# A third plain pair ahead of the seven-product pairs of each MLP, its blocks in other PSUM banks, and a later spread of the norm's roots

## The chip, the cores and the metric

The kernel runs on one core of a Trainium2 chip. The metric is the device time of one execution in microseconds, as the median of several runs. The engines are named as in the profile: PE (matrix products), PEld (its weight loads), DVE (vector), ACT (scalar), POOL (GpSimd) and SP (which here issues the loads).

## What is computed

A residual stream of 512 tokens by 1024 features goes through two layers. The first has a gated MLP mixer (gMLP), the second a forgetting attention (FoX), and each is followed by a channel MLP with a squared ReLU. Every sub-layer begins with an RMS norm. What the change touches is the channel MLP, which runs twice:

```python
def rms_norm(x, g):
    y = x * rsqrt(mean(x * x, axis=-1) + 1e-6)
    return y * g

def sqrelu_mlp(h, w1, w2):           # h 512x1024, w1 1024x4096, w2 4096x1024
    return square(relu(h @ w1)) @ w2

x = x + sqrelu_mlp(rms_norm(x, mlp_norm_g[i]), mlp_w1[i], mlp_w2[i])
```

## The kernel before

**Precision and layout.** The stream is kept transposed, as eight tiles `x[b]` of 128 features by 512 tokens. Each operand of a product is split into a rounded high part and a low rest, and each product is three matmuls (`mm3`: high by high, high by low, low by high), accumulated in one PSUM bank. A weight chunk of 128 by 1024 (512 KB) is loaded by SP into a `raw` buffer (three of them), copied to `wh` by ACT (line 85), and the rest `wl` is made by DVE (line 86); there are four `wh`/`wl` buffers. Class `Stream` does this ahead of use: `take()` of chunk i splits up to chunk i+3 and loads up to i+6, as far as buffers are free.

**The order.** Instructions are written in program order for all engines. A scheduler at build time simulates the engines and emits, per engine, a fixed order: an instruction that is not ready in that simulation can be passed by later ones that are. `keep_in_program_order` pins an instruction, and `issue_after` puts instructions of an engine behind a given one. On the chip each engine then goes through its own order and waits on semaphores.

**The norm.** `Norm.block` (lines 267 to 277) makes the split stream `xh`, `xl` without the root, and adds up the squares on POOL. `Norm.finish` (line 290) sums over features with eight small matmuls into `nps`, DVE makes `ms` (line 297) and POOL the power -1/2, `rstd` (line 299). `Norm.spread` (line 301) broadcasts `rstd` with eight small matmuls into bank `npb`, and ACT copies it to `rbc` (line 308). Since the root is a factor per token, the up products can run before it is known; `rbc` is needed only when their banks are read.

**The MLP** (line 454). The 4096 hidden features are 32 blocks of 128, in 16 pairs. Each pair takes two chunks of `w1`. The first pairs are plain: `up(f)` runs 24 matmuls of 512 columns for a block (`dense_a`), into bank `ph`. Then `squares(n)` reads both banks of a pair with `rbc` (line 512, DVE, into `zc`, of which there is one buffer), ACT squares (line 499) and copies to `zh` (line 502), and DVE makes `zl` (line 503). All other pairs run `up_pair` (line 515), a seven-product scheme of the Strassen and Winograd kind on a 2 by 2 split of features and tokens: seven products of 12 matmuls of 256 columns, in banks `da` and `bc`. It needs sums of token halves (`token_sums`: `th` by ACT, `tl` by DVE and POOL, lines 470 to 482) and sums of the pair's weights (`Stream._sums`: `ssum` with four POOL operations at lines 112 to 115, split into `sh` by ACT and `sl` by DVE). `down_blocks` (line 549) runs 12 matmuls of 512 columns per block into bank `po` (`psB`), from the `zh`, `zl` of two pairs, and DVE adds them to `x` (line 559).

`MLP_ORDER` lists three "up" entries, then for each of the pairs 3 to 15 an "up" and two "down" chunks, whose four blocks are laid between the four parts of `up_pair`, and the remaining down chunks. PSUM has four banks `psA`, three `psB` and one `psD` (`nps`, `npb`). Before the change, two pairs are plain, all four of their blocks stand in `psA`, and pair 2 is the first `up_pair`, without down blocks between its parts:

```python
phs = [up(0), up(1)]
nm.finish()
more = [up(2, True)]
nm.spread()
more.append(up(3, True))
zs[0] = squares(0, phs)
zs[1] = squares(1, more)
```

`True` pins the first matmul of the block, and the weight sums of pair 2 are put behind the last of the token sums on POOL (`sums_behind`).

Of the kernel before, what the change touches and what calls it, by code (L numbers as in the profile page):

```python
# [1 line left out]

# [9 lines left out]
ALU = mybir.AluOpType  # L12
# [31 lines left out]

PLAIN = 2
MLP_ORDER = [("up", n) for n in range(3)]
_down = [("down", g, m) for g in range(8) for m in range(4)]
for _n in range(3, 16):  # L50
# [4 lines left out]
class Stream:  # L55
# [6 lines left out]
    def __init__(self, nc, pool, chunks, bufs, ahead, load_ahead, halved=()):  # L62
        self.nc, self.pool, self.bufs = nc, pool, bufs
        self.chunks = [c if isinstance(c, tuple) else (c, None) for c in chunks]
        self.sums_pool = self.sums_behind = None
        self.ahead, self.load_ahead = ahead, load_ahead
        self.halved = halved
        self.raw, self.parts = {}, {}
        self.loaded = self.split = self.taken = 0
# [18 lines left out]
    def _split(self):  # L88
        nc, i = self.nc, self.split
        kind = self.chunks[i][1]  # L90
        t, n = self.raw[i] if kind == "first" else self.raw.pop(i)
        hi = self.pool.tile([P, CHUNK_COLS], F32R, tag="wh", name=f"wh{i}", bufs=self.bufs[1])
        lo = self.pool.tile([P, CHUNK_COLS], F32R, tag="wl", name=f"wl{i}", bufs=self.bufs[1])
        eng = nc.gpsimd if i in self.pooled else nc.vector
        pieces = [slice(n // 2, n)] if kind == "second" else self._pieces(i, n)
        for sl in pieces:
            self._parts(hi[:, sl], lo[:, sl], t[:, sl], eng)
        self.parts[i] = (hi, lo)
        if kind == "second":
            with self.sums_behind or nullcontext():  # L100
                self._sums(i, self.raw.pop(i - 1)[0], t)
            self.sums_behind = None
        self.split += 1

    def _sums(self, i, f, g):
# [35 lines left out]
def trunk(ctx: ExitStack, tc: tile.TileContext, A, out, stages=4):  # L141
    nc = tc.nc
    pe, dve, act, pool = nc.tensor, nc.vector, nc.scalar, nc.gpsimd
# [8 lines left out]
    def psA(name):  # L152
        return ps.tile([P, S], F32, tag="A", name=name, bufs=4)
# [23 lines left out]
    def mlp_chunks(w1, w2):  # L177
        r = []
        for kind, *at in MLP_ORDER:
            if kind == "down":  # L180
                r += [w2[at[0], at[1]]]
            elif at[0] < PLAIN:
                r += [w1[2 * at[0] + e] for e in range(2)]
# [21 lines left out]
    ws = Stream(nc, wp, chunks, bufs=(3, 4), ahead=3, load_ahead=3, halved=(0, 1))  # L205
# [46 lines left out]
    def mm3(dst, ah, al, bh, bl, start, stop, pin=False, more=False):  # L252
        first = mm(dst, ah, bh, start, False, more)
        if pin:
            tc.keep_in_program_order(first)
        mm(dst, ah, bl, False, False, more)
        mm(dst, al, bh, False, stop, more)
# [52 lines left out]
    def dense_a(dst, w, nm, pin=False):  # L310

        wh, wl = (t.rearrange("p (k m) -> p k m", m=P) for t in w)
        for k in range(KB):
            mm3(dst, wh[:, k], wl[:, k], nm.h[k], nm.l[k], k == 0, k == KB - 1, pin and k == 0)
# [26 lines left out]
    nm = Norm(0)  # L341
# [8 lines left out]
    with ExitStack() as st:  # L350
# [6 lines left out]
        for g in range(4):  # L357
            pv = [(psB if g == 1 and i < 3 else psA)(f"pv{g}_{i}") for i in range(NT)]
            for c in range(4):
                wh, wl = (t.rearrange("p (k n) -> p k n", k=2) for t in ws.take())  # L360
                for i in range(NT):
                    for kk in range(2):
                        k = 2 * c + kk
# [90 lines left out]
    def mlp(nm, done):  # L454
        HS = S // 2
        with ExitStack() as st:
# [1 line left out]
            ws.sums_pool = mp  # L458
            pad(mp, 32)

            def up(f, pin=False):
                ph = psA(f"ph{nm.n}_{f}")
                dense_a(ph, ws.take(), nm, pin)
                return ph


# [3 lines left out]
            def token_sums(k):  # L470
                xg, t = (mp.tile([P, 2, S], F32, tag=f"z{w}", name=f"t{w}{nm.n}_{k}", bufs=5) for w in "hl")
                for e in range(2):
                    act.activation(xg[:, e], x[k + 4 * e], AF.Copy, scale=gains[:, nm.n, k + 4 * e : k + 4 * e + 1])
                (b11, b12), (b21, b22) = ((xg[:, e, :HS], xg[:, e, HS:]) for e in range(2))
                t = t.rearrange("p a (b n) -> p (a b) n", b=2)
                dve.tensor_tensor(t[:, 0], b12, b11, op=ALU.subtract)
                dve.tensor_tensor(t[:, 2], b22, b12, op=ALU.subtract)
                tc.keep_in_program_order(pool.tensor_tensor(t[:, 1], b22, t[:, 0], op=ALU.subtract))
                last = tc.keep_in_program_order(pool.tensor_tensor(t[:, 3], b21, t[:, 1], op=ALU.subtract))
                act.activation(th[k], t, AF.Copy)  # L480
                dve.tensor_tensor(tl[k], t, th[k].bitcast(F32), op=ALU.subtract)
                return last

            def half(e, j):
                sl = slice(j * HS, (j + 1) * HS)
# [11 lines left out]
            def rectified(n, c):  # L497

                act.activation(c, c, AF.Square)
                h = mp.tile([P, 2, S], F32R, tag="zh", name=f"zh{nm.n}_{n}", bufs=5)  # L500
                l = mp.tile([P, 2, S], F32R, tag="zl", name=f"zl{nm.n}_{n}", bufs=5)
                act.activation(h, c, AF.Copy)
                dve.tensor_tensor(l, c, h.bitcast(F32), op=ALU.subtract)
                return h, l

            def squared(n):
                return mp.tile([P, 2, S], F32, tag="zc", name=f"zc{nm.n}_{n}", bufs=1)

            def squares(n, phs):
                c = squared(n)  # L510
                for e, ph in enumerate(phs):
                    dve.scalar_tensor_tensor(c[:, e], ph, 0.0, nm.rbc, op0=ALU.max, op1=ALU.mult)
                return rectified(n, c)
# [50 lines left out]
            zs = {}  # L564
            with tc.issue_after(nm.squared.ins):
                for k in range(4):
                    last = token_sums(k)
            ws.sums_behind = tc.issue_after(last.ins)
            phs = [up(0), up(1)]
            nm.finish()  # L570
            more = [up(2, True)]
            nm.spread()
            more.append(up(3, True))
            zs[0] = squares(0, phs)
            zs[1] = squares(1, more)
            at = 2
            while at < len(MLP_ORDER):
                kind, *arg = MLP_ORDER[at]
                at += 1
# [17 lines left out]
    if stages == 1:  # L597
        for b in range(KB):
            store(b)
        return  # L600
    fx = Norm(2)
    mlp(nxt, fx.block if stages > 2 else store)
    if stages == 2:
        return
    nm = fx
# [3 lines left out]
    with ExitStack() as st:  # L609
# [277 lines left out]
        last = nx3.block if stages > 3 else store  # L887
# [16 lines left out]
    if stages == 3:  # L904
        return
    mlp(nx3, store)


# [70 lines left out]
```

## Time and profile before

| | us |
|---|---|
| median of 3 runs | 1290.82 (1290.09 to 1290.98) |
| the profiled execution | 1290.49 |
| its span, first to last instruction | 1288.8 |
| PE busy | 1263.7 |
| DVE / ACT / POOL busy | 887.4 / 631.0 / 503.4 |

The profile is of one execution. Times within it count from the first instruction. An entry of the timeline has its start, its length, the engine, the line and the operation with its output and inputs, and in brackets the idle time ahead of it with what ended it. Matmuls are pipelined, so that the length of one is more than its share of time: the spacing of the starts is what counts. PEclk is the granted clock of TensorE, 1.00 being 2.4 GHz and 0.50 being 1.2 GHz.

### The profile page before, as it was taken

Reading aid. Unit: us, or ns where it says so; the run is one execution under the profiler, and the core shown is the slowest. Engines: PE = TensorE matmul, PEld = TensorE weight load, DVE = VectorE, ACT = ScalarE, POOL = GpSimd, SP = SyncE. Lnnn points to the kernel's source line nnn. Section 1 sums busy time; section 2 is a strip of 40 time slices with the busy share of each in tenths; the row PEclk is TensorE's granted clock in tenths of the full one; section 3 lists DMA queues with packets and bytes.
Section 4 is the critical chain, followed back from the end, with each engine's and each line's share of the span. In section 5 each row is a group of like instructions: output and inputs, shape, how many; then the busy total and the mean of one; then the engine's idle time right before and its main releaser. Section 6 shows DMA issues by size and latency. Waiting matters only on the chain.

```text
span 1288.8 us, 18536 instructions
## 1 busy us (share of the span) xinstructions
PE 1263.7 (98%) x7180; PEld 1118.5 (87%) x7180; DVE 887.4 (69%) x1212; ACT 631.0 (49%) x993; POOL 503.4 (39%) x423
## 2 busy tenths in 40 slices
PE   9999999998999999999999999999979999999998
PEld 8888888887999999998899899898869999999987
DVE  7347766688767676765536777777897867676763
ACT  7334333355534343443467687678465434444430
POOL 4209423027423232210657667666284422222200
PEclk9999999998999999999999999999989999999999
DMA  7332323222332333323223222223213333232321
GB/s 249 95 115 82 91 90 85 96 83 70 105 121 85 112 95 102 104 94 95 80 83 99 82 83 74 87 78 106 77 64 116 99 98 107 90 114 83 115 82 66
DMA packets 39608, 124.02 MB, mean 96 GB/s; under 512 B 4816, under 2 KB 5840, under 8 KB 39520
## 3 DMA queue, kind: packets, MB, share of 16 engines
q1 hardware_dynamic: 39232, 122.82, 30.4%
q8 instruction: 56, 0.92, 0.3%
q14 instruction: 32, 0.26, 0.1%
q10 hardware_dynamic: 288, 0.02, 0.0%
HBM read 120.69 MB, written 2.13 MB: 95 GB/s over the span
## 4 chain that ended last, share of the span: by engine, by line
PE 85%; DVE 8%; ACT 2%; POOL 2%; issue 1%; DMA 1%; POOLq 0%; ACTq 0%; DVEq 0%
PE po L245 34%; PE da L245 12%; PE bc L245 9%; PE pq L245 8%; PE pv L245 7%; PE pu L245 7%; DVE xl L273 2%; PE pg L245 2%; PE ot L245 2%; DVE wl L86 1%; DVE ee L811 1%; PE lg L245 1%; PE tp L250 1%; PE sp L428 1%; ACT wh L85 1%
## 5 line engine op out<-in xcount | busy, mean ns | idle before, releaser
L85 ACT ACTIVATE wh<-raw 128x1024 fp32r<-128x1024 f32 (+3 forms) x230 | 219.0, 953 | 276.6 <-PE po L245 86.5
L86 DVE TENSOR_TENSOR wl<-raw,wh 128x1024 fp32r<-128x1024 f32 (+1 forms) x178 | 255.0, 1444 | 50.9 <-ACT wh L85 50.5
L245 PE MATMUL po<-zl,wh 128*128 128x512 f32 x512 | 200.5, 392 | 0.0
L245 PE MATMUL po<-zh,wh 128*128 128x512 f32 x512 | 200.2, 391 | 0.0
L245 PE MATMUL po<-zh,wl 128*128 128x512 f32 x512 | 199.5, 390 | 0.0
L559 DVE TENSOR_TENSOR x<-x,po 128x512 f32<-128x512 f32 x128 | 87.3, 682 | 111.5 <-PE po L245 111.5
L86 POOL TENSOR_TENSOR wl<-raw,wh 128x768 fp32r<-128x768 f32 (+3 forms) x52 | 103.1, 1983 | 124.2 <-ACT wh L85 121.7
L112 POOL TENSOR_TENSOR ssum<-raw 128x512 f32<-128x512 f32 x28 | 40.7, 1453 | 261.1 <-DMA raw<-in_m_dram 242.4
L85 ACT ACTIVATE sh<-ssum 128x1024 fp32r<-128x1024 f32 x56 | 59.4, 1061 | 169.5 <-POOL ssum L113 121.7
L245 PEld LDWEIGHTS po<-zh,wl 128*128 128x128 f32 x512 | 96.2, 188 | 19.6
L245 PEld LDWEIGHTS po<-zh,wh 128*128 128x128 f32 x512 | 96.5, 188 | 18.0
L245 PEld LDWEIGHTS po<-zl,wh 128*128 128x128 f32 x512 | 96.6, 189 | 16.2
L245 PE MATMUL pq<-wh,xh 128*128 128x384 f32 (+2 forms) x256 | 88.4, 345 | 0.0
L412 POOL TENSOR_SCALAR vn<-v,mv,lnr 128x128 f32<-128x128 f32 x64 | 63.3, 1004 | 59.4 <-DVE vl L416 59.3
L245 PE MATMUL pq<-wh,xl 128*128 128x384 f32 (+2 forms) x256 | 83.1, 324 | 0.0
L245 PE MATMUL pq<-wl,xh 128*128 128x384 f32 (+2 forms) x256 | 82.7, 323 | 0.0
L86 DVE TENSOR_TENSOR sl<-ssum,sh 128x1024 fp32r<-128x1024 f32 x56 | 71.5, 1277 | 11.5 <-ACT sh L85 11.5
L114 POOL TENSOR_TENSOR ssum<-raw,ssum 128x512 f32<-128x512 f32 x28 | 39.3, 1404 | 75.7 <-DVE sl L86 75.4
L115 POOL TENSOR_TENSOR ssum<-raw,raw 128x512 f32<-128x512 f32 x28 | 63.5, 2269 | 1.2 <-DVE sl L86 1.2
L245 PE MATMUL da<-th,sl 128*128 128x256 f32 x224 | 63.4, 283 | 0.0
L245 PE MATMUL da<-tl,sh 128*128 128x256 f32 x224 | 63.4, 283 | 0.0
L245 PE MATMUL da<-th,sh 128*128 128x256 f32 x224 | 63.1, 282 | 0.0
(212 smaller groups left out, 3517.9 us busy)
## 6 DMA issues: line engine op xcount, KB each, us to landing
raw<-in_m_dram SPq DMA_DIRECT2D x128, 512.0 KB, 3.6
raw<-in_gw_u_dram SPq DMA_DIRECT2D x16, 512.0 KB, 3.5
raw<-in_gw_o_dram SPq DMA_DIRECT2D x16, 512.0 KB, 3.5
raw<-in_fw_qkv_dram SPq DMA_DIRECT2D x20, 384.0 KB, 3.0
raw<-in_gw_v_dram SPq DMA_DIRECT2D x14, 512.0 KB, 3.8
raw<-in_fw_g_dram SPq DMA_DIRECT2D x8, 512.0 KB, 3.4
cb<-cd SPq DMA_DIRECT2D x16, 256.0 KB, 3.3
raw<-in_fw_o_dram SPq DMA_DIRECT2D x8, 512.0 KB, 3.5
```

The lines of the kernel that those rows point to most:

```text
L85: self.nc.scalar.activation(hi, t, AF.Copy)
L86: eng.tensor_tensor(lo, t, hi.bitcast(F32), op=ALU.subtract)
L112: tt(s12[:, 0], a21, a22, op=ALU.add)
L114: tt(s43[:, 0], a12, s12[:, 1], op=ALU.subtract)
L115: tt(s43[:, 1], a11, a21, op=ALU.subtract)
L245: ins = pe.matmul(dst, a, b, start=start, stop=stop, skip_group_check=more)
L250: placed(pe.transpose(dst, src, ident[: src.shape[0], : src.shape[0]]), 256)
L273: dve.scalar_tensor_tensor(l, x[b], gcol, h.bitcast(F32), op0=ALU.mult, op1=ALU.subtract)
L412: pool.tensor_scalar(vn[:, i], v[i][:, cb * P : (cb + 1) * P], mv[:, i, 0:1], lnr[:, i : i + 1], op0=ALU.subtract, op1=ALU.mult)
L428: pe.matmul(dst, vh[:, 2 * c + i], wide, start=True, stop=False)
L559: dve.tensor_tensor(x[b], x[b], pt, op=ALU.add)
L811: dve.tensor_scalar(ees[i], ees[i], rc[:, i : i + 1], None, op0=ALU.mult)
```

## The change

Three pairs are plain instead of two; pair 2 takes plain blocks 4 and 5 in place of the seven products, and its two weight chunks need no sums. The blocks of pair 1 (2 and 3) stand in two of the three `psB` banks, those of pairs 0 and 2 in `psA`. `finish` stays behind block 1; `spread` moves from behind block 2 to behind block 4. The pins on blocks 2 and 3 and the order between weight sums and token sums go. `squares` runs for all three pairs behind block 5. The first `up_pair` is then pair 3, which has down blocks between its parts.

```diff
-PLAIN = 2
+PLAIN = 3
...
         if kind == "second":
-            with self.sums_behind or nullcontext():
-                self._sums(i, self.raw.pop(i - 1)[0], t)
-            self.sums_behind = None
+            self._sums(i, self.raw.pop(i - 1)[0], t)
...
-            def up(f, pin=False):
-                ph = psA(f"ph{nm.n}_{f}")
-                dense_a(ph, ws.take(), nm, pin)
+            def up(f, bank):
+                ph = bank(f"ph{nm.n}_{f}")
+                dense_a(ph, ws.take(), nm)
                 return ph
...
-                last = tc.keep_in_program_order(pool.tensor_tensor(t[:, 3], b21, t[:, 1], op=ALU.subtract))
+                tc.keep_in_program_order(pool.tensor_tensor(t[:, 3], b21, t[:, 1], op=ALU.subtract))
...
-                    last = token_sums(k)
-            ws.sums_behind = tc.issue_after(last.ins)
-            phs = [up(0), up(1)]
+                    token_sums(k)
+            phs = [[up(0, psA), up(1, psA)]]
             nm.finish()
-            more = [up(2, True)]
+            phs.append([up(2, psB), up(3, psB)])
+            phs.append([up(4, psA)])
             nm.spread()
-            more.append(up(3, True))
-            zs[0] = squares(0, phs)
-            zs[1] = squares(1, more)
-            at = 2
+            phs[2].append(up(5, psA))
+            for n in range(PLAIN):
+                zs[n] = squares(n, phs[n])
+            at = PLAIN
```

## Rows read from the trace of the kernel before

**Rows 1.** The page: span, then busy time of PE, then the chain by engine.
```profile
span 1288.8 us, 18536 instructions
...
PE 1263.7 (98%) x7180; PEld 1118.5 (87%) x7180; DVE 887.4 (69%) x1212; ACT 631.0 (49%) x993; POOL 503.4 (39%) x423
...
PE 85%; DVE 8%; ACT 2%; POOL 2%; issue 1%; DMA 1%; POOLq 0%; ACTq 0%; DVEq 0%
```

**Rows 2.** Waits of PE, longest first: total us, times, longest.
```profile
PE npb L245 <- POOL rstd L299: 11.6, 2, 5.8
PE tp L250 <- DVE ptl L846: 5.1, 4, 1.9
```

**Rows 3.** Timeline of PE, first MLP.
```profile
296.03 0.95 PE L245 MATMUL nps<-ones,sqs 128*128 128x2 f32 x8
...
302.19 0.39 PE L245 MATMUL ph<-xh,wl 128*128 128x512 f32 x1
308.40 2.08 PE L245 MATMUL npb<-ident,rstd 128*128 128x128 f32 x8 [5.82 <-POOL rstd L299]
310.13 0.77 PE L245 MATMUL ph<-xh,wh 128*128 128x512 f32 x1
...
316.34 0.28 PE L245 MATMUL da<-th,wh 128*128 128x256 f32 x1
...
329.29 0.40 PE L245 MATMUL po<-zh,wh 128*128 128x512 f32 x1
```

**Rows 4.** Timeline of PE, second MLP.
```profile
954.08 0.39 PE L245 MATMUL ph<-xh,wl 128*128 128x512 f32 x1
960.27 2.07 PE L245 MATMUL npb<-ident,rstd 128*128 128x128 f32 x8 [5.81 <-POOL rstd L299]
...
968.23 0.28 PE L245 MATMUL da<-th,wh 128*128 128x256 f32 x1
...
978.41 0.28 PE L245 MATMUL da<-xh,wl 128*128 128x256 f32 x1
978.81 0.39 PE L245 MATMUL bc<-xh,sh 128*128 128x256 f32 x1
```

**Rows 5.** Stretches of the first MLP: length, busy (count) by engine, PEclk, DMA.
```profile
302.60:308.40 5.80, 0.00 (x1) 0.00 (x1) 5.22 (x5) 1.06 (x1) 5.80 (x4) 0.68 0.00 0
308.40:310.13 1.73, 1.73 (x9) 1.73 (x9) 0.85 (x1) 0.00 (x0) 1.73 (x1) 0.50 0.89 268
310.13:316.34 6.21, 6.21 (x27) 5.08 (x26) 4.30 (x4) 3.01 (x4) 4.35 (x4) 0.89 0.28 94
```

**Rows 6.** Timelines of DVE and POOL, first MLP, around the root.
```profile
303.51 0.15 DVE L297 TENSOR_SCALAR ms<-nps 128x4 f32<-128x4 f32 x1
...
304.67 2.24 POOL L113 TENSOR_TENSOR ssum<-ssum,raw 128x512 f32<-128x512 f32 x1
306.87 1.48 POOL L299 TENSOR_TENSOR rstd<-ms,mhalf 128x4 f32<-128x4 f32 x1
```

**Rows 7.** The chain in order of time: 24 matmuls of 512 and of 256 columns.
```profile
162.61 5.44 PE pu L245 x24
...
316.50 2.87 PE da L245 x24
```

**Rows 8.** Timeline of PE in the FoX stage: `npb` without a wait.
```profile
648.07 1.05 PE L245 MATMUL npb<-ident,rstd 128*128 128x128 f32 x8
648.88 0.43 PE L245 MATMUL pq<-wh,xh 128*128 128x400 f32 x1
```

**Rows 9.** Timeline of DVE, first MLP: chunk 4's rest, then the squares.
```profile
299.59 1.75 DVE L86 TENSOR_TENSOR wl<-raw,wh 128x1024 fp32r<-128x1024 f32 x1
...
314.52 1.27 DVE L512 SCALAR_TENSOR_TENSOR zc<-ph,rbc 128x512 f32<-128x512 f32 x2
318.01 1.45 DVE L503 TENSOR_TENSOR zl<-zc,zh 128x1024 fp32r<-128x1024 f32 x1 [2.22 <-ACT zh L502]
...
324.54 1.22 DVE L503 TENSOR_TENSOR zl<-zc,zh 128x1024 fp32r<-128x1024 f32 x1
```

**Rows 10.** Timeline of POOL, first MLP: the weight sums of pair 3.
```profile
311.07 1.30 POOL L112 TENSOR_TENSOR ssum<-raw 128x512 f32<-128x512 f32 x1 [0.70 <-DMA raw<-in_m_dram]
...
317.08 1.30 POOL L114 TENSOR_TENSOR ssum<-raw,ssum 128x512 f32<-128x512 f32 x1
```

**Rows 11.** Groups by line: splits of a whole chunk and of sums.
```profile
L86 DVE TENSOR_TENSOR wl<-raw,wh 128x1024 fp32r<-128x1024 f32 x146 | 227.8, 1574 | 49.8 <-ACT wh L85 49.4
...
L86 DVE TENSOR_TENSOR sl<-ssum,sh 128x1024 fp32r<-128x1024 f32 x56 | 71.5, 1277 | 11.5 <-ACT sh L85 11.5
...
L85 ACT ACTIVATE sh<-ssum 128x1024 fp32r<-128x1024 f32 x56 | 59.4, 1061 | 169.5 <-POOL ssum L113 121.7 <-issue 17.6 <-POOL ssum L112 14.2
```

More of the change, by code (lines that the diff above doesn't have):

```diff
@@ L1 @@
-from contextlib import ExitStack, nullcontext
+from contextlib import ExitStack
 import concourse.bass as bass
@@ L64, in __init__ @@
         self.chunks = [c if isinstance(c, tuple) else (c, None) for c in chunks]
-        self.sums_pool = self.sums_behind = None
+        self.sums_pool = None
         self.ahead, self.load_ahead = ahead, load_ahead
@@ L478, in token_sums @@
                 tc.keep_in_program_order(pool.tensor_tensor(t[:, 1], b22, t[:, 0], op=ALU.subtract))
-                last = tc.keep_in_program_order(pool.tensor_tensor(t[:, 3], b21, t[:, 1], op=ALU.subtract))
+                tc.keep_in_program_order(pool.tensor_tensor(t[:, 3], b21, t[:, 1], op=ALU.subtract))
                 act.activation(th[k], t, AF.Copy)
                 dve.tensor_tensor(tl[k], t, th[k].bitcast(F32), op=ALU.subtract)
-                return last
             def half(e, j):
```

## The prediction

> **What bounds the kernel now.** I read the page first. PE is busy for 1263.7 of 1288.8 us and holds 85% of the chain that ended last [rows 1]. So only two things move the time: what PE has to issue, and the some 25 us in which it stands still. The waits of PE come next: the largest is that of the `npb` matmuls on POOL's `rstd`, 11.6 us in two waits of 5.8, more than twice the next [rows 2]. The timeline of PE shows where they are, one in each MLP: the last matmul of block 2 starts at 302.19, and the eight of `npb` at 308.40 after 5.82 us idle [rows 3]; in the second MLP it is 954.08 and 960.27 [rows 4]. The reader should see that this wait has a tail. By the stretches, the granted clock falls to its lower level, 1.2 GHz, in the idle time; the `npb` matmuls run at 0.50 throughout, and block 3 at a mean of 0.89 [rows 5].
>
> Why the root is late: `nps` is issued at 296.03 [rows 3], but DVE reaches `ms` only at 303.51, behind its part of the token sums, and POOL reaches `rstd` only at 306.87, behind a weight sum that ends at 306.91, so that it is there at 308.35 [rows 6]. Nothing on PE between blocks 2 and 3 covers this.
>
> **The change, part by part.**
>
> *Later spread.* With the spread behind block 4, blocks 3 and 4 stand ahead of `npb`. Undisturbed, 24 matmuls of 512 columns take 5.44 us [rows 7], so `npb` is due at 302.42 (302.19 and one spacing of 0.227) + 2 x 5.44 = 313.30. `rstd` would have been there at 308.35 by its old path, 4.9 us before. The wait goes, and its clock tail with it. Before, from 302.42 to the first `da` matmul at 316.34, PE spent 13.92 us on `npb` and block 3 [rows 3]; the second MLP gives 968.23 - 954.31 = 13.92 too [rows 4]. Undisturbed, the same work takes 0.81 (`npb` from 648.07 to 648.88 [rows 8]) + 5.44 = 6.25 us. Gain: 7.67 us in each MLP, of which 5.82 is the wait and the rest mostly the slow clock.
>
> *Pair 2 plain.* It adds 48 matmuls of 512 columns, 48 x 0.2267 = 10.88 us, and removes 84 of 256, 84 x 2.87/24 = 10.05 us [rows 7]. Price: 0.83 us in each MLP. The shorter form is dear for its columns: 0.1196 us for 256 is more than half of 0.2267 for 512. The Trainium skill ("TensorE: Matmul & The Clock Gate", Back-to-back issue gap) gives the spacing at the full clock as columns over 2.4 GHz plus some 2.5 ns, and by it the pairs would be estimated at 10.36 and 9.17 us. The price would be 1.19, and the gain of both MLPs 0.7 us smaller; the rows differ from the page in both widths, and they decide.
>
> *Other engines.* Pair 2 loses four POOL sums, two `sh` of 1.06 us on ACT and two `sl` of 1.28 on DVE, and all that reads `da` and `bc`; it gains the second half of a `wl` split (1.57 whole) and two bank reads of 0.64 [rows 9, 11]. All three engines have less to do, and none of this sets PE's pace, so I count it as nothing. If that cover failed, it would show as the waits among the rivals. The bytes loaded and SP's issues are the same; a plain chunk gives its `raw` buffer back when it is split, where one with sums keeps it until POOL has summed, so loads can only come earlier.
>
> *Block 4's and 5's weights.* Chunk 4's `wl` was ready at 301.34 [rows 9], needed at 307.86. Chunk 5 follows it by one split, needed at 314.11. Nothing.
>
> *Banks.* Blocks 2 and 3 in `psB` leave two `psA` banks for blocks 4 and 5; the first `up_pair` needs the banks of blocks 0 and 1. Before, the first bank was read by 315.16 (one of two in 1.27 us from 314.52 [rows 9]), 5.03 us after block 3 began at 310.13 [rows 3]. Block 5 takes 5.44 us. `bc` follows `da` by 2.87 us. A margin of 0.4 us: cost nothing, and at most the 0.6 us of one read.
>
> *Pins and the order on POOL removed.* The first sums are now those of pair 3, whose second chunk comes later than the token sums end, so the removed order should not matter: nothing. Without pins, blocks 2 and 3 may fill small gaps where block 1 waits for the last `xl`; I bound that gain by a microsecond over both MLPs and count none.
>
> *Squares.* Three go through the one `zc` buffer. From the start of block 3, `zl` of pair 1 took until 324.54 + 1.22 = 325.76, so 15.6 us [rows 3, 9]. Pair 2's unfilled 10.05 us covered it. Now the first `up_pair` has down blocks in its program order, but the emitted order can leave them behind: before, even pair 3's first products were put ahead of the down blocks, whose first matmul came at 329.29, 3.5 us after `zl` was there [rows 3]. Between zero and the full wait worked out below (5.7), I take 0.3 us in each MLP, the size of the one gap there is near (978.41 to 978.81, less one spacing of 0.12 [rows 4]).
>
> *Sum.* In each MLP -7.67 + 0.83 + 0.3 = -6.54; both, -13.1 us. Against the profiled execution, 1290.49 (its span 1288.8 and 1.7 around it), that is 1277.4. The median of the runs is 0.3 above that execution, so I predict 1277.7, 1.0% faster.
>
> **Rivals.**
>
> *A. As summed.* 1275 to 1281.5: down by a microsecond or two for filled gaps, up by up to 2 us of new waits in each MLP. For it: a margin of 4.9 us on `rstd`, and the trace's order, which passes work that isn't ready.
>
> *B. The wait moves to the first down block.* If the down blocks stay in written order, the 7th matmul of the first (the first to read pair 1) is due 5.44 + 2.87 + 1.36 = 9.67 us after block 5 starts, and the chain of squares takes 15.4 to 15.6 from there: a wait of 5.7, with up to 0.8 for the clock behind it. That gives back 6.5 of 6.84, and the time is about 1290. Half of it gives 1284. For it: DVE has no idle time of weight in this stretch (5.22 of 5.80 us [rows 5]), so squares have been late there already. Against: the order of the trace, above.
>
> *C. Slower: the root behind the sums of pair 3 on POOL.* No order is written between them. Those sums ran from 311.07, when the chunk came, to 318.38 [rows 10]. If `rstd` stood behind all four with the load no earlier than before, it would end at 318.38 + 1.48 = 319.9; `npb`, due at 313.30, would wait 6.6 us and bring back the clock tail of 1.7. Each MLP would be 6.6 + 1.7 - 6.84 = 1.4 worse: 1293.7. It decides from a `rstd` that ends after 318.5 (no gain); over 0.2% slower needs 319.8. For it: `rstd` did stand behind a sum before [rows 6]. Against: `ms` is ready at 303.7, and the chunk cannot be there until its `raw` buffer is free of chunk 4, at 301.3, and loaded. The Trainium skill ("TensorE: Matmul & The Clock Gate", architectural detail on engine queues) states that ScalarE, VectorE and GpSimdE take their queues strictly in order, so a root emitted behind the sums could not pass them; no row here shows it passing.
>
> *D. The move does nothing.* The order comes from a simulation, and could put `npb` ahead of block 3 as before. Then only the price of the plain pair is left, 2 x 0.83: 1292.5, which is within 0.2%.
>
> **From cases to numbers.** About 0.2% (2.6 us) is what a measurement of this kernel can tell from no change. Chances: A 0.77; B in part (1281.5 to 1288) 0.10, B in full 0.05; C 0.05; D 0.03. Faster by over 0.2% is A and partial B, 0.87; within 0.2% is full B and D, 0.08; slower is C, 0.05. For 8 in 10 the range goes from 1275, below which little of A lies, into partial B to 1286.5; it leaves out some 0.03 below and 0.15 above.
>
> **What would show it.** In the changed profile the list of PE's waits should have no `npb` on `rstd`; the granted clock should stay at 1.00 through both starts; from the last matmul of block 2 to the first `da`, PE should take 3 x 5.44 + 0.81 = 17.1 us; `rstd` should end before block 4 does; each MLP should be some 6.5 us shorter, and all else as it was. I am wrong if a new wait of PE stands at the first `po` (B), at `npb` (C, D), or at the first `da` for a bank; or if the new emission order moves other stages, the FoX stage above all, which these sums leave alone.

## The result, and the profile after

The changed kernel takes 1277.12 us (median of four runs, 1276.96 to 1278.73) against 1290.74 (the runs of the table above and one more): a ratio of 0.9898, with a 95% interval of 0.9881 to 0.9915. Predicted were 1277.7, and 1275 to 1286.5 as the range. The profiled execution's span is 1275.3 us, 13.5 less than before.

The page after: PE is busy for 1.6 us less and the span is 13.5 shorter, so that nearly all of the gain is idle time and not work.

```profile
span 1275.3 us, 18354 instructions
...
PE 1262.1 (99%) x7108; PEld 1114.0 (87%) x7108; DVE 877.2 (69%) x1206; ACT 624.9 (49%) x981; POOL 484.7 (38%) x415
...
PE 89%; DVE 6%; ACT 2%; issue 1%; POOL 1%; DMA 1%; DVEq 0%; ACTq 0%; POOLq 0%
```

The waits of PE: `npb` on `rstd`, 11.6 us in [rows 2], is gone. A `po` that waits for `zl` is new.

```profile
PE tp L248 <- DVE ptl L843: 3.6, 4, 1.9
PE po L243 <- DVE zl L500: 1.3, 1, 1.3
```

The timeline of PE in the first MLP, which answers to [rows 3]. Blocks 3 and 4 follow block 2 without a gap; from the last matmul of block 2 and one spacing, 302.88, to the first `da` at 320.12 it is 17.24 us, where 17.1 was predicted. In the second MLP it is 17.25 us, from 946.36 to 963.61.

```profile
302.65 0.39 PE L243 MATMUL ph<-xh,wl 128*128 128x512 f32 x1
302.88 0.39 PE L243 MATMUL ph<-xh,wh 128*128 128x512 f32 x1
...
320.12 0.28 PE L243 MATMUL da<-th,wh 128*128 128x256 f32 x1
```

The same stretch with the busy time of each engine, to hold against [rows 5]: the granted clock is 1.00, and DVE has idle time, 9.76 busy of 17.24.

```profile
302.88:320.12 17.24, 17.24 (x81) 14.41 (x80) 9.76 (x12) 7.48 (x9) 7.87 (x5) 1.00 0.49 150
```

Timelines of DVE and POOL around the root, as in [rows 6]. POOL has no weight sum ahead of the root, and `ms` comes a little earlier, so that `rstd` ends at 305.03 instead of 308.35, in a stage that begins 0.46 later.

```profile
302.85 0.15 DVE L295 TENSOR_SCALAR ms<-nps 128x4 f32<-128x4 f32 x1
...
303.08 1.95 POOL L297 TENSOR_TENSOR rstd<-ms,mhalf 128x4 f32<-128x4 f32 x1 [2.37 <-DVE ms L295]
```

**Where the 13.5 us came from.** I cut the span at the `nps` matmuls, which stand at 296.03, 642.80 and 947.91 before and at 296.49, 636.49 and 941.56 after. In the second MLP seven matmuls of block 2 (1.59 us) now run ahead of `nps`, around the place where PE waits for the last `xl`; I count them with the MLP, here and in every kernel below. The first stretch, from `nps` through the first MLP to FoX's `nps`, shrank from 346.77 to 340.00 (-6.77). FoX and the start of the second MLP shrank by 1.63, the rest, from 340.86 to 335.32, by 5.54, and the stage ahead of all this grew by 0.46. Some 1.4 of the 1.63 comes from one meeting of two engines in FoX, where the change edits nothing; the last section shows it.

### The profile page after: what moved, and what is told of

Same layout as the page of the kernel before. It is cut to its first block, busy times and chain, and to the rows that moved or that the text cites. A ratio compares the mean times of both kernels' runs of the same rounds, so it can differ in the third digit from the quotient of the medians.

```text
span 1275.3 us, 18354 instructions
## 1 busy us (share of the span) xinstructions
PE 1262.1 (99%) x7108; PEld 1114.0 (87%) x7108; DVE 877.2 (69%) x1206; ACT 624.9 (49%) x981; POOL 484.7 (38%) x415
## 4 chain that ended last, share of the span: by engine, by line
PE 89%; DVE 6%; ACT 2%; issue 1%; POOL 1%; DMA 1%; DVEq 0%; ACTq 0%; POOLq 0%
PE po L243 36%; PE da L243 11%; PE bc L243 9%; PE pq L243 8%; PE pv L243 8%; PE pu L243 7%; PE ph L243 3%; PE pg L243 2%; PE ot L243 2%; DVE xl L271 1%; PE lg L243 1%; PE tp L248 1%; PE sp L426 1%; DVE ee L808 1%; DVE y L726 1%
## 5 line engine op out<-in xcount | busy, mean ns | idle before, releaser
L110 POOL TENSOR_TENSOR ssum<-raw 128x512 f32<-128x512 f32 x26 | 35.5, 1364 | 268.6 <-DMA raw<-in_m_dram 256.8
L85 ACT ACTIVATE sh<-ssum 128x1024 fp32r<-128x1024 f32 x52 | 55.2, 1061 | 164.5 <-POOL ssum L111 95.8
L86 DVE TENSOR_TENSOR sl<-ssum,sh 128x1024 fp32r<-128x1024 f32 x52 | 65.9, 1268 | 18.2 <-ACT sh L85 18.1
L243 PE MATMUL da<-th,sl 128*128 128x256 f32 x208 | 58.9, 283 | 0.0
L243 PE MATMUL da<-tl,sh 128*128 128x256 f32 x208 | 58.8, 283 | 0.0
L243 PE MATMUL pv<-wh,xh 128*128 128x512 f32 (+1 forms) x160 | 58.0, 372 | 0.7 <-ACT wh L85 0.7
L243 PE MATMUL pv<-wl,xh 128*128 128x512 f32 (+1 forms) x160 | 58.7, 368 | 0.0
```

Source lines behind the costliest of these rows:

```text
L85: self.nc.scalar.activation(hi, t, AF.Copy)
L86: eng.tensor_tensor(lo, t, hi.bitcast(F32), op=ALU.subtract)
L110: tt(s12[:, 0], a21, a22, op=ALU.add)
L243: ins = pe.matmul(dst, a, b, start=start, stop=stop, skip_group_check=more)
```

## The experiments

Each was timed in five rounds beside the kernel before on the same chip; the ratio is to that kernel. The median of the kernel before lay between 1290.74 and 1292.01 us in these sittings, so where two experiments differ by little I compare the two MLP stretches of their profiles, cut as above. Lines of code are those of the changed kernel if nothing else is said.

**Two plain pairs, later spread.** Does the third plain pair do anything but cost?

```diff
-PLAIN = 3
+PLAIN = 2
...
             phs.append([up(2, psB), up(3, psB)])
-            phs.append([up(4, psA)])
             nm.spread()
-            phs[2].append(up(5, psA))
```

> Two plain pairs as before, but blocks 2 and 3 in the down blocks' banks and the roots spread behind block 3; pair 2 is a seven-product pair again. Theory (the gain is cover for the root, the third plain pair only costs): the changed kernel's 1277.1 less 2 x 0.83 for the plain pair, 1275.5; up to 1 us more if rstd, behind pair 2's weight sums on POOL as before (308.35 against a due time of 307.86), is still 0.5 late in each MLP. Rival (the gain comes from the third plain pair, whose missing sums free POOL and DVE): the wait on rstd is back or moves to the first da or po, and at most half of the 13.6 us gain is left, 1283 or more.

Measured: 1284.75, ratio 0.9950 (0.9937 to 0.9962). Half of the gain is gone, and the rival's range holds. The timeline of POOL shows where it begins. Without the order that the change removed, sums of pair 2 (`ssum`) run ahead of and between the token sums (`tl`).

```profile
288.50 2.29 POOL L110 TENSOR_TENSOR ssum<-raw 128x512 f32<-128x512 f32 x1
...
293.89 1.48 POOL L111 TENSOR_TENSOR ssum<-ssum,raw 128x512 f32<-128x512 f32 x1
295.33 0.93 POOL L476 TENSOR_TENSOR tl<-th,tl 128x256 f32<-128x256 f32 x1
296.22 1.46 POOL L112 TENSOR_TENSOR ssum<-raw,ssum 128x512 f32<-128x512 f32 x1
```

Their splits (`sl`) then stand ahead of `ms` and of `tl` on DVE:

```profile
300.52 1.76 DVE L86 TENSOR_TENSOR sl<-ssum,sh 128x1024 fp32r<-128x1024 f32 x1
...
303.88 1.75 DVE L86 TENSOR_TENSOR sl<-ssum,sh 128x1024 fp32r<-128x1024 f32 x1
...
307.24 0.15 DVE L295 TENSOR_SCALAR ms<-nps 128x4 f32<-128x4 f32 x1
```

PE waits in turn for the root and for `tl`:

```profile
309.47 1.16 PE L243 MATMUL npb<-ident,rstd 128*128 128x128 f32 x8 [1.00 <-POOL rstd L297]
312.53 0.39 PE L243 MATMUL da<-tl,wh 128*128 128x256 f32 x1 [0.72 <-DVE tl L479]
...
958.51 1.16 PE L243 MATMUL npb<-ident,rstd 128*128 128x128 f32 x8 [2.59 <-POOL rstd L297]
962.12 0.58 PE L243 MATMUL da<-tl,wh 128*128 128x256 f32 x1 [0.82 <-DVE tl L479]
```

The sums' place on POOL by itself is not what costs most of this: in the later experiment with two plain pairs and `rbc` first, POOL has the very same order, and the time is 1275.68.

**Three plain pairs, early spread.** Does the place of the spread matter, once the third plain pair is there?

```diff
-            phs.append([up(2, psB), up(3, psB)])
-            phs.append([up(4, psA)])
+            phs.append([up(2, psB)])
             nm.spread()
-            phs[2].append(up(5, psA))
+            phs[1].append(up(3, psB))
+            phs.append([up(4, psA), up(5, psA)])
```

> Three plain pairs, roots spread behind block 2 in program order, as before; the emitted order puts the spread behind 7 matmuls of block 3 in the first MLP and behind 11 in the second. Theory as predicted (the old path of rstd, ready 5.9 us after block 2 ends, holds): PE waits 4.3 and 3.4 us for rstd, plus a clock tail of up to 1.7 each, so 1284 to 1288. Rival (with pair 2's weight sums gone, POOL makes the root 3.3 us earlier, so the place of the spread hardly matters): waits of 0 to 1.5 us, 1276 to 1279.

Measured: 1278.74, ratio 0.9905 (0.9892 to 0.9919). The theory, with the old path of the root, falls. PE waits 0.47 and 1.72 us for `rstd`, not 4.3 and 3.4. The root now ends 2.17 and 4.31 us behind the end of block 2, where it was 5.93 and 5.91 before: the weight sums that are missing had held it up on POOL and DVE. That accounts for 5.4 of the 11.6 us of wait. Another 4.1 are covered, since the emitted order put 7 and 11 matmuls of block 3 ahead of the spread, and 2.2 are left. So about half of the old wait was the root's place in the queues of POOL and DVE, and half was lack of cover.

**Three plain pairs, spread behind block 3.**

```diff
             phs.append([up(2, psB), up(3, psB)])
-            phs.append([up(4, psA)])
             nm.spread()
-            phs[2].append(up(5, psA))
+            phs.append([up(4, psA), up(5, psA)])
```

> Three plain pairs, roots spread behind block 3 instead of block 4. Theory: no wait on rstd (due 5.4 us after block 2, there after 2.6), and the squares begin 5.4 us earlier, so that the 1.35 us wait of the first down block on zl in the second MLP goes: 1275.5 to 1277. Rival (that wait comes from DVE being behind for other reasons): 1277 to 1278, with the wait still there.

Measured: 1280.08, ratio 0.9913 (0.9899 to 0.9926), outside what either said. No wait for the root, but in the second MLP the first `po` waits 2.25 us for `zh`. The timeline of ACT there shows why. `npb` was done at 953.3, but `rbc` runs at 960.39, behind two `sh` that wait for POOL's weight sums.

```profile
957.53 1.06 ACT L85 ACTIVATE sh<-ssum 128x1024 fp32r<-128x1024 f32 x1 [7.51 <-POOL ssum L111]
958.90 1.06 ACT L85 ACTIVATE sh<-ssum 128x1024 fp32r<-128x1024 f32 x1 [0.32 <-POOL ssum L112]
959.87 0.61 ACT L85 ACTIVATE wh<-raw 128x512 fp32r<-128x512 f32 x1
960.39 0.58 ACT L306 ACTIVATE rbc<-npb 128x512 f32<-128x512 f32 x1
```

**Banks swapped.**

```diff
-            phs.append([up(2, psB), up(3, psB)])
-            phs.append([up(4, psA)])
+            phs.append([up(2, psA), up(3, psA)])
+            phs.append([up(4, psB)])
             nm.spread()
-            phs[2].append(up(5, psA))
+            phs[2].append(up(5, psB))
```

> As the changed kernel, but pair 1 stands in psA and pair 2 in psB. Theory (banks cost nothing as long as two psA banks are read before the first seven-product pair needs them, and PE has other work): the first down blocks find one free psB bank until pair 2 is squared, the emitted order puts pair 4's products in between, and the time is 1277 to 1280. Rival (the placing of pair 1 in the down blocks' banks is what makes the change work): new waits of PE of 2 to 5 us in each MLP, 1281 to 1287.

Measured: 1277.63, ratio 0.9897 (0.9882 to 0.9912): the changed kernel's time. Which pair stands in the down blocks' banks hardly matters; the one wait at a `po` is 1.97 us instead of 1.35, and by the profiles the two MLPs take 0.7 us more in all.

**Two plain pairs, root ahead of the sums.** This is the first experiment with one more order: pair 2's `_sums` run in `tc.issue_after` of the root's POOL instruction.

```diff
             nm.finish()
+            ws.sums_behind = tc.issue_after(nm.root.ins)
```

> Two plain pairs, banks and spread as in the run before with two plain pairs, but pair 2's weight sums are put behind the root on POOL. Theory (that run lost because pair 2's sums went ahead of the token sums on POOL and their sl ahead of ms on DVE, so that rstd, tl and sl were late; without that the third plain pair only costs): rstd is there at about 305, no wait at npb; the sums end near 314, which may leave up to 1 us of wait for sl in each MLP: 1275.5 to 1278. Rival (with pair 2 on seven products there is too little time for its sums whatever their order): waits of 3 to 4 us for sl or tl in each MLP, 1282 to 1285.

Measured: 1285.88, ratio 0.9953 (0.9941 to 0.9966): no better than the first experiment, and above what either said. The root is in time, but now `rbc` stands behind `sh` on ACT, at 312.37 and 961.97 (spread at 308.20 and 954.83), so that the banks are read late. PE waits for a bank (`zc`) and for the copies of `da` by ACT:

```profile
PE da L245 <- DVE zc L511: 2.5, 2, 2.1
PE da L245 <- ACT sl L525: 2.3, 2, 1.1
...
PE bc L245 <- DVE sl L86: 0.9, 1, 0.9
```

**Spread behind block 3, `rbc` first.** If `sh` on ACT is what holds up `rbc`, putting the sums' ACT copies behind it should turn the loss of the third experiment into a gain.

```diff
             nm.spread()
+            ws.sums_behind = tc.issue_after(nm.copied.ins)      # the ACT copy to rbc
             phs.append([up(4, psA), up(5, psA)])
```

> Three plain pairs, spread behind block 3 as in the run of that name, and the ACT and POOL work on pair 3's weight sums put so that its ACT copies (sh) come behind rbc on ACT. Theory (rbc was late there because it stood behind an sh that waited 7.5 us for POOL): rbc comes about 7 us earlier in the second MLP, squares too, the 2.25 us wait at the first po goes, 1275.5 to 1277. Rival (DVE and ACT are behind anyway): the wait at po or a new one for sl stays, 1278 to 1280.

Measured: 1275.28, ratio 0.9872 (0.9858 to 0.9885). All waits of PE at the start of both MLPs but one of 0.47 us for the last `xl` are gone. The theory holds, and `rbc` runs 7 us earlier:

```profile
953.18 0.60 ACT L308 ACTIVATE rbc<-npb 128x512 f32<-128x512 f32 x1
957.64 1.06 ACT L85 ACTIVATE sh<-ssum 128x1024 fp32r<-128x1024 f32 x1 [3.86 <-POOL ssum L113]
```

By the profiles the second MLP takes 333.73 us instead of 337.97, and the first the same. The two kernels have the same instructions and the same order on POOL. `sh` moved on ACT and with it `sl` on DVE, and behind them some of the squares and of the down matmuls.

**The wait filled with work that nobody reads**, in the kernel before.

```diff
             more = [up(2, True)]
+            fill = psB(f"fill{nm.n}")
+            for k in range(24):
+                tc.keep_in_program_order(mm(fill, nm.h[k % KB][:, :P], nm.l[k % KB], True, True))
             nm.spread()
```

> The kernel before, with 24 matmuls of 512 columns that nothing reads put between block 2 and the spread in each MLP. Theory (the wait is 5.8 us of idle time and costs 1.7 us more through the slow clock behind it): the fillers take 5.44 us, npb waits 0 to 0.5 us more, npb and block 3 run at the full clock, and the time falls by about 3 us in all, 1287 to 1288. Rival (the clock tail is not real or comes whatever PE does in the wait): no change, 1290 to 1291, or slower.

Measured: 1289.97, ratio 0.9988 (0.9979 to 0.9998). The clock stays at 1.00, and `npb` and block 3 together take their undisturbed time:

```profile
309.50:315.70 6.20, 6.20 (x31) 5.29 (x32) 3.93 (x3) 2.49 (x3) 4.25 (x3) 1.00 0.50 169
...
316.44 0.39 PE L245 MATMUL da<-th,wh 128*128 128x256 f32 x1 [0.35 <-DVE zc L512]
```

But from the end of block 2 (303.44, 953.40) to the first `da` (316.44, 966.99) it is 13.00 and 13.59 us, only 0.92 and 0.33 less than 13.92. Now `da` waits 0.35 and 0.95 us for the bank of block 0, and PE waits again behind it. The slow clock had been cover for the bank read. So the clock tail is real, but to take it away alone is worth little. The gain in time is half of what I expected, and by the profiles none of it is in the MLPs: the first is 0.15 us shorter and the second 0.53 longer, while FoX is 1.77 shorter for another reason (last section).

**Pair 8 plain too**, in the middle of each MLP. In this kernel the second up block of pair 8 and the first down blocks behind it take each other's weight chunk; instructions, shapes and bytes are as meant, so that it serves for the time, but it does not compute the reference's function.

```diff
-            elif at[0] < PLAIN:
+            elif at[0] < PLAIN or at[0] == 8:
...
-                for _ in up_pair(*arg):
+                for _ in (plain_pair if arg[0] == 8 else up_pair)(*arg):
```

> The changed kernel with pair 8 plain as well, in the middle of each MLP with its down blocks around it, where PE does not wait. Theory (a plain pair costs 0.83 us of PE, by the spacings): 1277.1 + 1.7 = 1278.8. Rival 1 (by the skill's spacings, 1.19 a pair): 1279.5. Rival 2 (the other engines' work that falls away gives time back): 1277 or less.

Measured: 1279.21, ratio 0.9900 (0.9887 to 0.9914). By the same cuts as above, with 7 matmuls of block 2 ahead of `nps` here too, the first MLP takes 340.74 us against 340.00, and the second 336.02 against 335.32: 0.74 and 0.70 a pair. Predicted were 0.83; the 1.19 by the spacings of the Trainium skill ("TensorE: Matmul & The Clock Gate", Back-to-back issue gap) is too much.

**Two plain pairs, `rbc` first.** The call for the sums of pair 2 stands behind the spread, and their ACT copies `sh` go behind `rbc`. On POOL the sums keep the place that they had in the first experiment, ahead of the root.

```diff
-PLAIN = 3
+PLAIN = 2
...
+            ws.hold = True                 # pair 2's _sums are put off
             phs = [[up(0, psA), up(1, psA)]]
             nm.finish()
             phs.append([up(2, psB), up(3, psB)])
-            phs.append([up(4, psA)])
             nm.spread()
-            phs[2].append(up(5, psA))
+            with tc.issue_after(nm.copied.ins):
+                ws.sum_held()
```

> Two plain pairs, pair 1 in the down blocks' banks, spread behind block 3, and the work on pair 2's weight sums issued behind the spread, its ACT copies behind rbc. Theory (both two-plain runs lost by order alone: first the root behind the sums, then rbc behind an sh that waited for them; the third plain pair itself only costs): rbc by 309.5 in the first MLP, no wait for a bank, at most 1 us for sl in each MLP; the fastest so far, 1275.3 less 1.7 plus 0 to 2, so 1273.6 to 1275.6. Rival (pair 2 on seven products leaves no time for its weight sums, the third plain pair buys that time): its first sums are not split when bc needs them, waits of 3 us or more in each MLP, 1280 or more.

Measured: 1275.68, ratio 0.9884 (0.9868 to 0.9901), 9 to 10 us faster than the two earlier kernels with two plain pairs. Time for pair 2's sums was there. What the first experiment lacked is the order of `sh` on ACT and of `sl` behind it on DVE; POOL's order is the same in both, and only from pair 2 on does PE's differ. One wait of 1.55 us for the root is left, in the second MLP.

**The changed kernel, `rbc` first.** The same lines (`hold` set behind pair 1, `sum_held` behind `spread`), with three plain pairs and the spread behind block 4.

> The changed kernel, spread behind block 4 as it is, with pair 3's weight sums issued behind the spread and their ACT copies behind rbc. Theory (the 1.35 us wait at a first po comes from rbc standing behind sh): rbc about 2 us earlier in the second MLP, the wait goes: 1275.5 to 1276.5. Rival (what gained in the run with the spread behind block 3 was the earlier spread): wait stays, or sl becomes late for bc, 1277 to 1279.

Measured: 1275.72, ratio 0.9886 (0.9871 to 0.9900). `rbc` runs at 958.65 instead of 960.66, and no `po` waits; by the profiles the second MLP takes 333.73 us instead of 335.32. PE and POOL have the same order in both kernels, and on ACT and DVE only two `sh` and two `sl` of each MLP moved. That wait of the changed kernel was thus `rbc` behind `sh`, too. The changed kernel first, then this one:

```profile
958.22 1.06 ACT L85 ACTIVATE sh<-ssum 128x1024 fp32r<-128x1024 f32 x1 [0.30 <-POOL ssum L112]
...
960.66 0.57 ACT L306 ACTIVATE rbc<-npb 128x512 f32<-128x512 f32 x1
```

```profile
958.65 0.60 ACT L312 ACTIVATE rbc<-npb 128x512 f32<-128x512 f32 x1
959.15 1.05 ACT L85 ACTIVATE sh<-ssum 128x1024 fp32r<-128x1024 f32 x1
```

**The root behind the sums**, the rival that would have made the change slower.

```diff
             phs.append([up(4, psA)])
+            with tc.issue_after(ws.summed.ins):      # last of pair 3's four POOL sums
+                nm.root()                            # the power -1/2, no longer in finish()
             nm.spread()
```

> The changed kernel with the root's POOL operation put behind all four weight sums of pair 3, as in the rival that would have made the change slower. Theory (the sums end at 311.4 and 958.2 in the changed kernel's trace, npb is due at 313.8 and 957.2): no wait in the first MLP, 2.4 us in the second, where rbc stood at 960.7 anyway: 1278 to 1280. Rival (as priced in the prediction, with the chunk as late as before): 6.6 us and a slow clock in each MLP, 1290 or more.

Measured: 1280.01, ratio 0.9916 (0.9901 to 0.9931). The orders of PE, ACT and DVE are those of the changed kernel. The first MLP has no wait, although the root now ends at 313.07, 4.7 us later than in the kernel before; the second has one of 2.79 us:

```profile
311.05 2.02 POOL L301 TENSOR_TENSOR rstd<-ms,mhalf 128x4 f32<-128x4 f32 x1
...
960.61 1.67 PE L243 MATMUL npb<-ident,rstd 128*128 128x128 f32 x8 [2.79 <-POOL rstd L301]
```

## Why the prediction was right, point by point

**The wait and its clock tail** (-7.67 in each MLP) and **the plain pair** (+0.83): 17.24 us from block 2 to `da` against the 17.1 of the sum, at full clock. The plain pair's price by itself is 0.70 to 0.74 at pair 8. At its own place it is 0.85: the first MLP takes 339.17 us with two plain pairs and 340.02 with three, both with `rbc` first and without a wait of PE.

**Why the wait went** was told only in part. I gave `rstd` its old time, 308.35, and the later spread the credit. The later spread does what I said: in the last experiment it covers, in the first MLP, a root that ends over 10 us behind block 2, without a wait. But in the changed kernel the root also came earlier, 2.15 and 4.31 us behind block 2 instead of 5.93 and 5.91, because pair 2's sums had left its queues; with two plain pairs and the root put ahead of their sums it ends as early, at 304.92 in the first MLP. That alone, with the early spread, leaves 2.2 us of the 11.6, and its two MLPs take 1.1 us more than those of the changed kernel. The two causes overlap, so that the gain can't be shared out between them.

**"None of this sets PE's pace"**, of POOL, DVE and ACT having less to do, is therefore the step that was too strong, though it cost the sum nothing. The third plain pair is not only a price. Without it, and without the order between weight sums and token sums that the change removed, a spread one block later keeps half of the gain. But what it gives is order and not time: with `sh` put behind `rbc`, two plain pairs do as well. Two plain pairs with the old order kept and only the spread moved were not run.

**The squares** (0.3 in each MLP): zero and 1.35. Case B was there in its smallest form, and with `rbc` put ahead of `sh` on ACT it goes.

**Banks, pins, chunks 4 and 5** cost nothing; the swapped banks bear out the first. The first bank was read by 316.65 and `da` began at 320.12, so that the margin was 3.5 us and not 0.4. That block 2 fills the gap at the last `xl` was bounded at a microsecond; that wait fell from 0.74 to 0.48.

**The slower rival** was priced too high. It gave the sums the load of before. In the changed kernel pair 3's chunk is there by 305.40 instead of 311.07, its sums end 7 us earlier (311.41 instead of 318.38), and the root behind them costs 2.9 us in all instead of 16. That its buffer came free earlier, since pair 2's chunks wait for no sums, fits this but was not tried by itself.

**The sum.** -13.1 predicted and -13.5 in the profile: the two MLPs gave -12.3 (-6.77 and -5.54), and FoX 1.4 that the sum knew nothing of. The agreement to half a microsecond is in part luck.

## What to carry to other kernels

When a chain of small operations over several engines is late, look at what stands ahead of each of them in its engine's queue before covering it with more work: here each link stood behind something else, `ms` on DVE behind a token sum's split, `rstd` on POOL behind a weight sum, and `rbc` on ACT behind `sh`, which itself waited for POOL. Work that makes room in a queue and work that covers a wait look alike in the time, and only experiments that do one without the other tell them apart. If the order is emitted by a simulation, an order written for one long-waiting operation can be worth more than moving its consumer: three kernels with it took 1275.3 to 1275.7 us, below the changed kernel in every median. Their intervals meet or overlap its own, but by the profiles their two MLPs take 1.5 to 1.6 us less.

## What the runs showed of the hardware

In FoX of the kernel before, four DVE operations of line 811 (`ee` times a column, 128 to 512 wide) take 2.95 us while POOL splits a weight chunk, and PE then waits 1.95 us:

```profile
687.54 2.95 DVE L811 TENSOR_SCALAR ee<-ee,rc 128x128 f32<-128x128 f32 x4
...
688.37 1.84 POOL L86 TENSOR_TENSOR wl<-raw,wh 128x768 fp32r<-128x768 f32 x1 [0.38 <-ACT wh L85]
```

After the change the same four take 1.28 us, though POOL's split begins 0.82 us behind their start as it did before (0.83), and PE waits 0.42:

```profile
681.41 1.28 DVE L808 TENSOR_SCALAR ee<-ee,rc 128x128 f32<-128x128 f32 x4
...
682.23 2.14 POOL L86 TENSOR_TENSOR wl<-raw,wh 128x768 fp32r<-128x768 f32 x1 [0.75 <-ACT wh L85]
```

It is the last of the four, the one 512 wide, that differs. Before, it starts 0.01 us behind POOL's split and takes 2.11 us; after, it starts 0.03 ahead of it and takes 0.48:

```profile
688.38 2.11 DVE L811 TENSOR_SCALAR ee<-ee,rc 128x512 f32<-128x512 f32 x1
```

```profile
682.20 0.48 DVE L808 TENSOR_SCALAR ee<-ee,rc 128x512 f32<-128x512 f32 x1
```

The filled kernel, whose FoX code is that of before, takes 1.27 us for the four. In each of the twelve other profiles the last one starts 0.03 to 0.04 us ahead of POOL and takes 0.47 to 0.49 us. So hundredths of a microsecond at this meeting go with 1.5 us of PE, and nothing that the change was meant to do bears on them. That the filled kernel is some 1.5 us faster by its ratio, though its MLPs are not, suggests that the kernel before often meets POOL in this way; with one profile of each kernel it is not shown. In the slow case DVE ends at 690.49, 0.28 behind POOL; in the fast one POOL's split is the longer (2.14 against 1.84 us). The Trainium skill ("GPSIMD Engine Reference", Specifications) says that GpSimd shares its SBUF interfaces with VectorE, with contention for some kinds of DVE instructions. The rows agree that they hinder each other, and the 2.11 us look as if the operation that came second waited for the other to end; that was not tried by itself.
